# Low parts of the latent up-projection weights on VectorE, and every second head's diagonal blocks copied by ScalarE

## The chip, the cores and the metric

The kernel runs on one core of a Trainium2 chip. The metric is device time in microseconds (us); the time before is the median of three runs. Engines are called by their names or as the profile shortens them: TensorE (PE, and PEld for its weight loads), VectorE (DVE), ScalarE (ACT), GpSimd (POOL), SyncE (SP), which issues the loads.

## What is computed

Three transformer layers over 256 tokens of width 1024, in float32. Layer 1 mixes a gated linear recurrence, a gated linear attention and a block attention. Layers 2 and 3 (one function, called twice) each run three mixers side by side: a delta-rule recurrence (RWKV-7), a dilated local attention, and a latent attention (MLA). Every layer ends with an output projection and a gated FFN of width 2816. The lines that the change touches belong to these two parts of the reference:

```python
def step(state, inp):                      # delta rule, one token after another
    r_t, w_t, k_t, v_t, kk_t, b_t = inp
    sa = jnp.einsum('bhvk,bhk->bhv', state, kk_t)
    state = (state * w_t[:, :, None, :] - sa[..., None] * b_t[:, :, None, :]
             + v_t[..., None] * k_t[:, :, None, :])
    return state, jnp.einsum('bhvk,bhk->bhv', state, r_t)
...
q = (rms_norm_2(cq, q_norm_g) @ w_uq)      # latent attention: up-projections
kv = (rms_norm_2(ckv, kv_norm_g) @ w_ukv)
```

## The kernel before

**Weights.** Every large weight comes from memory as a float32 tile (`wraw`, three buffers, loads on SyncE's queue) and is split in two: ScalarE writes a rounded high part (`whi`, line 293), and the low part `wlo = wraw - whi` is made by VectorE (line 295) or, where the caller passes `G`, by GpSimd (line 297). Both parts have five buffers. A product is three matmuls: high by high, low by high, high by low. With 266 such splits the weights' path is a steady load of ScalarE and VectorE. GpSimd makes the low parts in `latent` and of the first three weights of each `out_proj`.

**The mixer of layers 2 and 3.** `layer2` writes the recurrence, the dilated and the latent attention as generators, and `lay` traces them in the order of the string `PLAN2`: `i` is the chain of the recurrence (`inverses`), `d` the dilated attention, `l` the latent attention, `c`, `v`, `o`, `u` the rest of the recurrence. The traced order gives each instruction its priority. A scheduler then gives each engine one fixed list of instructions; it takes the earliest in the traced order among those that it holds ready at that moment. Each engine works through its list strictly in order, and an instruction that waits holds up all behind it. PLAN2 begins `iciiiiiididlilli`: the setting up of the four weights of `latent` (in the first `l`) is traced after the block copies and before the first step of `solve`.

**The chain of the recurrence.** `inverses` scales keys and queries by decays: `kk` is multiplied by the learning rate (line 1248, VectorE, 128x512), `be` and `ka` follow (1249, 1256). `pairs` multiplies `be` with keys and queries on TensorE (line 1286), for two heads at a time and in two PSUM banks `r`; VectorE copies the masked result to `LN` (line 1291), after GpSimd has set it to zero (line 1290). Then the 32x32 blocks on the diagonal of each head's matrix are copied side by side into `Nd` (line 1264): four blocks for each of four heads, each copy 32 partitions x 64 elements, all by GpSimd. `solve` inverts the unit triangular matrices: line 1038 masks `Nd` into `Zd`, line 1039 transposes it to `Xd`, and then 32x32 products on TensorE (line 1035), ScalarE copies (1044) and masked VectorE copies (1048) double the inverted block size step by step.

**Beside it.** TensorE works in the same stretch on the dilated attention's projection (lines 472 to 475, the second half of the tokens) and then on the latent attention (lines 327 to 329). The high parts of three of the latent weights wait for buffers that the dilated projection still reads.

Of the kernel before, what the change touches and what calls it, by code (L numbers as in the profile page):

```python
# [13 lines left out]
AF = mybir.ActivationFunctionType  # L14
# [231 lines left out]
def tile_kernel(ctx: ExitStack, tc: tile.TileContext, a: dict, out: bass.AP, taps: dict = {}):  # L246
    nc = tc.nc
    V, A, G, PE = nc.vector, nc.scalar, nc.gpsimd, nc.tensor
# [9 lines left out]
    def bank(tag):  # L258
        return psum.tile([128, 512], F32, name="ps" + tag, tag="ps" + tag, bufs=BANKS[tag])
# [10 lines left out]
    def A1(name, shape, dt=F32):  # L270
        return T1(name, shape, dt, "a")
# [9 lines left out]
    def raw_weight(ap):  # L281
        raw = wpool.tile([128, ap.shape[1]], F32, name="wraw", tag="wraw", bufs=WB[0])
        nc.sync.dma_start(raw, ap)
        return raw

    def weight(ap, E=None):

        return split(raw_weight(ap), E)

    def split(raw, E=None):  # L290
        hi = wpool.tile([128, raw.shape[1]], F32R, name="whi", tag="whi", bufs=WB[1])
        lo = wpool.tile([128, raw.shape[1]], F32R, name="wlo", tag="wlo", bufs=WB[1])
        A.activation(hi, raw, AF.Copy)  # L293
        if E is None:
            V.tensor_sub(lo, raw, hi)  # L295
        else:
            E.tensor_tensor(lo, raw, hi, op=ALU.subtract)
        return hi, lo
# [26 lines left out]
    def mm3(o, xs, ws, start, stop):  # L325

        PE.matmul(o, xs[0], ws[0], start=start, stop=False)  # L327
        PE.matmul(o, xs[1], ws[0], start=False, stop=False)  # L328
        PE.matmul(o, xs[0], ws[1], start=False, stop=stop)  # L329
# [16 lines left out]
    def C(name):  # L346
        return found[name]
# [159 lines left out]
    def attention(score, bias, scale, v, h0, nh, dh, mixT, k0):  # L507


        n = 128 // dh  # L510

        def out_of(o, j):
            return o, j == 0, j == n - 1

        for i in range(0, nh, n):
            o = bank("o")[:, :256]
            for j in range(n):
                p = bank("s")
                score(h0 + i + j, p)
                softmax_head(p, bias(h0 + i + j), scale, v(h0 + i + j), *out_of(o, j))  # L520
                if j < n - 1:
                    yield
            m = [mx[:, k0 + i // n] for mx in mixT]
            A.activation(m[0], o, AF.Copy)
            V.tensor_sub(m[1], o, m[0])
            yield
# [170 lines left out]
    def halves(p):  # L697
        return p.rearrange("p (c t) -> p c t", c=2)

    def heads(ap, n):  # L700
        return ap.rearrange("p (h d) -> p h d", h=n)

    def hd(h, n=64):
        return slice(h * n, (h + 1) * n)
# [301 lines left out]
    def rotate(dst, src, nh, r, t, j0):  # L1006

        cb = rope["cos"][:, t, j0:j0 + r].unsqueeze(1).to_broadcast([128, nh, r])
        sb = rope["sin"][:, t, j0:j0 + r].unsqueeze(1).to_broadcast([128, nh, r])
        t1, t2 = src[:, :, :r], src[:, :, r:2 * r]  # L1010
        u = [heads(T0(f"ro{i}", [128, 128], 1)[:, :nh * r], nh) for i in range(4)]
        V.tensor_tensor(u[0], t1, cb, op=ALU.mult)
        V.tensor_tensor(u[1], t2, sb, op=ALU.mult)
        V.tensor_tensor(u[2], t1, sb, op=ALU.mult)
        V.tensor_tensor(u[3], t2, cb, op=ALU.mult)
        V.tensor_tensor(dst[:, :, :r], u[0], u[1], op=ALU.subtract)
        V.tensor_tensor(dst[:, :, r:2 * r], u[2], u[3], op=ALU.add)
# [135 lines left out]
    def recurrent(l, W, hT, mixT, last):  # L1153

        n = Names()
# [22 lines left out]
        def inverses():  # L1178
# [80 lines left out]
            for hp in range(2):  # L1259
                n.LN += pairs(n.be, hp, "LN", "r")  # L1260
                for h in (2 * hp, 2 * hp + 1):
                    for b in range(4):
                        bs = hd(b, 32)
                        G.tensor_copy(Nd[bs, :, h], n.LN[h][bs, :, 0, bs])
                yield
            Z = mix.tile([128, 8, 128], F32, name="Z", tag="Z", bufs=1)
            n.Z = Z.rearrange("p (c h) t -> p c h t", c=2)
# [14 lines left out]
        def pairs(src, hp, name, tag):  # L1282
            ps, ds = [bank(tag), bank(tag)], []
            for c in range(2):
                for j in range(2):
                    PE.matmul(ps[j][:, hd(c, 256)], src[hd(j), 2 * hp + c],
                              n.AR[hd(j), 2 * hp + c].rearrange("p a t -> p (a t)"), start=True, stop=True)
            for j in range(2):
                d = T2(name, [128, 2, 2, 128])
                G.memset(d, 0.0)  # L1290
                V.copy_predicated(d.rearrange("p b a t -> p b (a t)"), C("si").unsqueeze(1).to_broadcast([128, 2, 256]),
                                  halves(ps[j]))
                ds.append(d)
            return ds
# [70 lines left out]
        def outputs():  # L1365
# [59 lines left out]
            for t in range(2):  # L1425
                finish(t)
                yield

        return rest(), inverses(), values(), operands(), outputs()

    def dilated(l, W, hT, mixT, dv):
# [25 lines left out]
        yield from attention(score, lambda h: C("dil"), 0.125, lambda h: (dv[0][:, h], dv[1][:, h]), 0, 4, 64, mixT, 2)  # L1457

    def latent(l, mixT, cq, ckv, krT):
        wq = [[v.rearrange("p (k c) -> p k c", k=2) for v in weight(a[f"wuq_{l}"][:, s0:s0 + n], G)]  # L1460
              for s0, n in ((0, 1024), (1024, 512))]
        wk = [weight(a[f"wkv_{l}"][:, hd(i, 512)], G) for i in range(2)]
        room = [big.tile([128, 4, 512], F32, name=n, tag=n) for n in ("hTl", "hTh")]
        room = [v[:, i] for v in room for i in range(4)]
        take = lambda: halves(room.pop())
        qr = [take(), take()]
        for h in range(2):
            G.memset(qr[h][hd(1 - h)], 0.0)
        cv = []
        for t in range(2):  # L1470
            ts = hd(t, 128)
            p = bank("p")
            for k in range(2):
                mm3(p[:, :256], (cq[0][:, k, ts], cq[1][:, k, ts]), (wq[1][0][:, k], wq[1][1][:, k]), k == 0, k == 1)
            q = A1("qrt", [128, 256])
            rotate(heads(q, 4), heads(p[:, :256], 4), 4, 32, t, 8)
            pt = bank("t")
            for i in range(2):
                PE.transpose(pt[:, hd(i, 128)], q[:, hd(i, 128)], ident)
            for h in range(2):  # L1480
                V.tensor_copy(qr[h][hd(h), :, ts], heads(pt[hd(h), :256], 2))
            yield
            p = bank("p")
            mm3(p, (ckv[0][:, ts], ckv[1][:, ts]), wk[1], True, True)
            cv.append(room.pop())
            A.activation(cv[-1], p, AF.Copy)
            yield
        parts = []
        for h2 in range(2):
            p = bank("p")  # L1490
            for j in range(2):
                o, ws = p[:, hd(j, 256)], hd(2 * h2 + j, 128)
                for k in range(2):
                    wh, wl = wq[0][0][:, k, ws], wq[0][1][:, k, ws]
                    PE.matmul(o, wh, cq[0][:, k], start=(k == 0), stop=False)
                    PE.matmul(o, wh, cq[1][:, k], start=False, stop=False)
                    PE.matmul(o, wl, cq[0][:, k], start=False, stop=(k == 1))
            qn = take()
            V.tensor_copy(qn, halves(p))
            yield  # L1500
            p = bank("p")
            for j in range(2):
                o, ws = p[:, hd(j, 256)], hd(2 * h2 + j, 128)
                PE.matmul(o, wk[0][0][:, ws], ckv[0], start=True, stop=False)
                PE.matmul(o, wk[0][0][:, ws], ckv[1], start=False, stop=False)
                PE.matmul(o, wk[0][1][:, ws], ckv[0], start=False, stop=True)
            kn = take()
            A.activation(kn, halves(p), AF.Copy)

            parts.append((qn, kn))  # L1510
            yield
        for h2, (qn, kn) in enumerate(parts):

            def score(h, p):
                for q0, o, n in ((0, 0, 128), (128, 128, 256)):
                    PE.matmul(p[:, o:o + n], qn[:, h % 2, q0:q0 + 128], kn[:, h % 2, :n], start=True, stop=False)
                    PE.matmul(p[:, o:o + n], qr[h % 2][:, h2, q0:q0 + 128], krT[:, :n], start=False, stop=True)

            yield from attention(score, lambda h: C("causal"), 192.0 ** -0.5,
                      lambda h: (cv[0][:, hd(h, 128)], cv[1][:, hd(h, 128)]), 2 * h2, 2, 128, mixT, 4 + 2 * h2)  # L1520
# [59 lines left out]
```

## Time and profile before

| | |
|---|---|
| median of 3 runs | 1007.76 us (1007.62 to 1007.81) |
| profiled execution | 1007.09 us |
| its span, first to last instruction | 1004.9 us |
| busy: PE, DVE, ACT, POOL | 962.8, 655.0, 549.6, 88.5 us |
| granted TensorE clock, mean | 0.996 |

Busy times are sums over the span. The profile also has, for any stretch, the list of instructions of one engine in order of time with the idle time before each and what ended it, the busy time of all engines by stretch, and the chain of work that ended last, followed back from the end.

### The profile page before, as it was taken

What the parts mean: (1) busy time and instruction counts of PE and PEld (TensorE: products, weight loads), DVE (VectorE), ACT (ScalarE), POOL (GpSimd) and SP (SyncE); (2) the same over time, 40 slices, a digit from 0 to 9 for tenths busy, and PEclk for the clock granted to TensorE, in tenths of its full rate; (3) what the DMA queues carried; (4) which work ended last, traced back from release to release, by engine and by line L of the source; (5) the groups of instructions that cost most, each with busy time, mean ns of one, the idle gap of its engine ahead of it and who ended that gap; (6) DMA issues with size and microseconds to landing.
All of it is one profiled execution on the core that took longest, in us unless ns stands there. A gap on an engine that the chain in (4) does not pass through costs nothing.

```text
span 1004.9 us, 16830 instructions
## 1 busy us (share of the span) xinstructions
PE 962.8 (96%) x6551; PEld 817.7 (81%) x6551; DVE 655.0 (65%) x1212; ACT 549.6 (55%) x995; POOL 88.5 (9%) x125
## 2 busy tenths in 40 slices
PE   4998989999999998999999999999799999999997
PEld 3987878888887976888788888889688878888886
DVE  4777676666676687566666667666856576666663
ACT  5467565555565564455655555557255465555652
POOL 0003110000001122400000000010530000000000
PEclk9999999999999999999999999999999999999999
DMA  7863546666674623214565667635321246666751
GB/s 244 258 209 90 155 143 217 187 188 189 209 227 141 187 91 108 78 45 147 191 195 189 187 189 237 211 98 161 96 78 51 85 146 196 188 190 188 216 175 42
DMA packets 48635, 161.35 MB, mean 161 GB/s; under 512 B 5683, under 2 KB 9004, under 8 KB 48556
## 3 DMA queue, kind: packets, MB, share of 16 engines
q1 hardware_dynamic: 48556, 160.28, 51.7%
q8 instruction: 51, 0.84, 0.3%
q14 instruction: 28, 0.23, 0.1%
HBM read 159.20 MB, written 1.06 MB: 159 GB/s over the span
## 4 chain that ended last, share of the span: by engine, by line
PE 79%; DVE 10%; DMA 4%; ACT 3%; issue 2%; POOL 2%; SPq 0%; POOLq 0%; ACTq 0%; DVEq 0%
PE psp L462 9%; PE psr L462 9%; PE psp L463 5%; PE psr L463 5%; PE psp L449 3%; PE pss L328 3%; PE pss L329 3%; PE psp L450 3%; PE pss L327 3%; PE psp L451 3%; DMA wraw<-in_ffn_dram 3%; ACT whi L293 2%; PE psp L475 2%; PE psp L473 2%; PE pst L327 2%
## 5 line engine op out<-in xcount | busy, mean ns | idle before, releaser
L295 DVE TENSOR_TENSOR wlo<-wraw,whi 128x1024 fp32r<-128x1024 f32 (+2 forms) x249 | 301.6, 1214 | 171.4 <-ACT whi L293 168.3
L293 ACT ACTIVATE whi<-wraw 128x1024 fp32r<-128x1024 f32 (+3 forms) x266 | 275.7, 1039 | 231.7 <-PE psp L462 70.2
L462 PE MATMUL psp<-hTh,whi 128*128 128x512 f32 x228 | 82.9, 396 | 0.0
L462 PE MATMUL psr<-hTh,whi 128*128 128x512 f32 x228 | 82.6, 396 | 0.0
L462 PE MATMUL psp<-hTl,whi 128*128 128x512 f32 x228 | 82.5, 395 | 0.0
L462 PE MATMUL psr<-hTl,whi 128*128 128x512 f32 x228 | 82.5, 395 | 0.0
L463 PE MATMUL psp<-hTh,wlo 128*128 128x256 f32 x228 | 64.2, 282 | 0.0
L463 PE MATMUL psr<-hTh,wlo 128*128 128x256 f32 x228 | 64.0, 281 | 0.0
L463 PE MATMUL psp<-hTl,wlo 128*128 128x256 f32 x228 | 63.9, 280 | 0.0
L463 PE MATMUL psr<-hTl,wlo 128*128 128x256 f32 x228 | 63.8, 280 | 0.0
L631 ACT ACTIVATE sl<-cr 128x256 f32<-128x256 f32 x57 | 23.8, 417 | 57.6 <-DVE cr L629 57.5
L462 PEld LDWEIGHTS psr<-hTl,whi 128*128 128x128 f32 x228 | 42.8, 188 | 10.2
L462 PEld LDWEIGHTS psp<-hTl,whi 128*128 128x128 f32 x228 | 42.7, 187 | 10.1
L462 PEld LDWEIGHTS psr<-hTh,whi 128*128 128x128 f32 x228 | 42.8, 188 | 10.0
L462 PEld LDWEIGHTS psp<-hTh,whi 128*128 128x128 f32 x228 | 42.8, 188 | 9.8
L463 PEld LDWEIGHTS psp<-hTh,wlo 128*128 128x128 f32 x228 | 43.0, 189 | 3.1 <-DVE wlo L295 0.7
L629 DVE TENSOR_TENSOR cr<-psr,cr 128x256 f32<-128x256 f32 x57 | 24.1, 423 | 30.8 <-ACT cr L628 30.8
L463 PEld LDWEIGHTS psp<-hTl,wlo 128*128 128x128 f32 x228 | 43.0, 189 | 0.1
L463 PEld LDWEIGHTS psr<-hTl,wlo 128*128 128x128 f32 x228 | 43.1, 189 | 0.0
L463 PEld LDWEIGHTS psr<-hTh,wlo 128*128 128x128 f32 x228 | 43.1, 189 | 0.0
L449 PE MATMUL psp<-hTh,whi 128*128 128x256 f32 x144 | 42.0, 292 | 0.1
L450 PE MATMUL psp<-hTl,whi 128*128 128x256 f32 x144 | 41.6, 289 | 0.0
(673 smaller groups left out, 2395.6 us busy)
## 6 DMA issues: line engine op xcount, KB each, us to landing
wraw<-in_ffn_dram SPq DMA_DIRECT2D x198, 512.0 KB, 4.0
wraw<-in_win_dram SPq DMA_DIRECT2D x48, 512.0 KB, 4.1
wraw<-in_wout_dram SPq DMA_DIRECT2D x24, 512.0 KB, 3.6
gain<-in_prow_dram SPq DMA_DIRECT2D x9, 512.0 KB, 4.4
wraw<-in_win_dram SPq DMA_DIRECT2D x8, 480.0 KB, 4.3
wraw<-in_win_dram SPq DMA_DIRECT2D x4, 272.0 KB, 3.1
tb<-bdr SPq DMA_DIRECT2D x4, 256.0 KB, 3.8
wraw<-in_wuq_dram SPq DMA_DIRECT2D x2, 512.0 KB, 3.5
```

Source lines behind the costliest of these rows:

```text
L293: A.activation(hi, raw, AF.Copy)
L295: V.tensor_sub(lo, raw, hi)
L327: PE.matmul(o, xs[0], ws[0], start=start, stop=False)
L328: PE.matmul(o, xs[1], ws[0], start=False, stop=False)
L329: PE.matmul(o, xs[0], ws[1], start=False, stop=stop)
L449: PE.matmul(o, wh, hT[0][:, k, :], start=(k == 0), stop=False)
L450: PE.matmul(o, wh, hT[1][:, k, :], start=False, stop=False)
L451: PE.matmul(o, wl, hT[0][:, k, :], start=False, stop=(k == KC - 1))
L462: PE.matmul(o, wt[0][:, k], hT[2][k // 4][:, k % 4], start=(k == 0), stop=False)
L463: PE.matmul(o[:, S:], wt[1][:, k], hT[0][:, k, :], start=False, stop=(k == KC - 1))
L629: V.tensor_tensor(cr[:, i], p[:, :S], cr[:, i], op=ALU.add)
L631: n_.silu = A.activation(sl[:, 0], cr[:, 0], AF.Silu)
```

## The change

```diff
                 for h in (2 * hp, 2 * hp + 1):
                     for b in range(4):
                         bs = hd(b, 32)
-                        G.tensor_copy(Nd[bs, :, h], n.LN[h][bs, :, 0, bs])
+                        if h % 2:
+                            A.activation(Nd[bs, :, h], n.LN[h][bs, :, 0, bs], AF.Copy)
+                        else:
+                            G.tensor_copy(Nd[bs, :, h], n.LN[h][bs, :, 0, bs])
...
     def latent(l, mixT, cq, ckv, krT):
-        wq = [[v.rearrange("p (k c) -> p k c", k=2) for v in weight(a[f"wuq_{l}"][:, s0:s0 + n], G)]
+        wq = [[v.rearrange("p (k c) -> p k c", k=2) for v in weight(a[f"wuq_{l}"][:, s0:s0 + n])]
               for s0, n in ((0, 1024), (1024, 512))]
-        wk = [weight(a[f"wkv_{l}"][:, hd(i, 512)], G) for i in range(2)]
+        wk = [weight(a[f"wkv_{l}"][:, hd(i, 512)]) for i in range(2)]
```

In each of layers 2 and 3, four low parts (one of 128x1024, three of 128x512) are made on line 295 by VectorE instead of line 297 by GpSimd, and the eight block copies of heads 1 and 3 are ScalarE copies; those of heads 0 and 2 stay on GpSimd. The products, buffers and loads are the same.

## Rows read from the trace of the kernel before

**Rows 1.** The page: busy time, share of the span, instructions of each engine.
```profile
PE 962.8 (96%) x6551; PEld 817.7 (81%) x6551; DVE 655.0 (65%) x1212; ACT 549.6 (55%) x995; POOL 88.5 (9%) x125
```
**Rows 2.** Busy time by stretch, all engines; then granted clock, DMA share, GB/s.
```profile
364.00:372.00 8.00, 7.27 (x37) 5.56 (x35) 5.19 (x8) 4.73 (x10) 4.75 (x3) 1.00 0.12 34
372.00:382.00 10.00, 7.50 (x55) 5.41 (x59) 8.85 (x23) 1.15 (x2) 6.84 (x21) 1.00 0.11 27
...
470.00:660.00 190.00, 189.04 (x993) 159.89 (x992) 124.96 (x176) 106.81 (x175) 4.02 (x7) 1.00 0.62 193
...
700.00:720.00 20.00, 16.82 (x204) 12.54 (x202) 15.74 (x31) 6.27 (x13) 13.01 (x24) 1.00 0.14 36
```
**Rows 3.** TensorE in time order, 364 to 396: start, duration; idle before, releaser.
```profile
372.96 1.14 PE L1286 MATMUL psr<-AR,be 64*128 64x256 f32 x8 [1.51 <-DVE be L1249]
...
376.02 1.74 PE L1286 MATMUL psr<-AR,be 64*128 64x256 f32 x8 [0.56 <-DVE LN L1291]
...
381.84 0.74 PE L1035 MATMUL psr<-Xd,LN 32*32 32x32 f32 x64 [0.98 <-DVE Xd L1039]
...
387.79 0.32 PE L1035 MATMUL psr<-Xd,LN 32*32 32x32 f32 x13 [1.71 <-issue]
```
**Rows 4.** VectorE in time order, 369 to 385.
```profile
369.13 2.48 DVE L1248 SCALAR_TENSOR_TENSOR kk<-kk,av 128x512 f32<-128x512 f32 x1
...
375.25 1.32 DVE L1291 COPY_PREDICATED LN<-i,psr 128x512 f32<-128x512 int32 x2
...
377.25 1.35 DVE L1291 COPY_PREDICATED LN<-i,psr 128x512 f32<-128x512 int32 x2
378.50 0.83 DVE L1448 COPY dqT<-pst 64x256 f32<-64x256 f32 x2
380.44 0.45 DVE L1038 COPY_PREDICATED Zd<-i,Nd 128x256 f32<-128x256 int32 x1 [1.11 <-POOL Nd L1264]
...
381.26 0.43 DVE L1039 STREAM_TRANSPOSE Xd<-Zd 128x256 f32<-128x256 f32 x1
381.62 2.08 DVE L1320 SCALAR_TENSOR_TENSOR r__3702<-r__3702,pcol,k__3602 128x256 f32<-128x256 f32 x2
...
384.21 0.45 DVE L1048 COPY_PREDICATED Zd<-i,psr 128x256 f32<-128x256 int32 x1 [0.43 <-PE psr L1035]
```
**Rows 5.** GpSimd in time order, 368 to 387.
```profile
368.42 2.65 POOL L297 TENSOR_TENSOR wlo<-wraw,whi 128x1024 fp32r<-128x1024 f32 x1 [2.67 <-ACT whi L293]
...
376.03 4.38 POOL L1264 COPY Nd<-LN 32x64 f32<-32x64 f32 x16 [0.85 <-DVE LN L1291]
380.49 2.93 POOL L297 TENSOR_TENSOR wlo<-wraw,whi 128x512 fp32r<-128x512 f32 x2
```
**Rows 6.** ScalarE in time order, 367 to 401.
```profile
367.29 1.05 ACT L293 ACTIVATE whi<-wraw 128x1024 fp32r<-128x1024 f32 x1
...
379.30 1.15 ACT L293 ACTIVATE whi<-wraw 128x512 fp32r<-128x512 f32 x2 [7.44 <-PE psp L475]
...
398.51 1.69 ACT L1054 ACTIVATE Z<-Zd 32x256 f32<-32x256 f32 x4 [1.75 <-DVE Zd L1048]
```
**Rows 7.** VectorE groups, whole span: count, busy us, mean ns, idle before.
```profile
L295 DVE TENSOR_TENSOR wlo<-wraw,whi 128x1024 fp32r<-128x1024 f32 x237 | 289.5, 1224 | 163.4 <-ACT whi L293 160.3
...
L306 DVE TENSOR_TENSOR wv<-wraw,wv 128x512 fp32r<-128x512 f32 x8 | 5.5, 684 | 0.2 <-ACT wv L305 0.2
...
L1248 DVE SCALAR_TENSOR_TENSOR kk<-kk,av 128x512 f32<-128x512 f32 x2 | 5.0, 2476 | 0.0
...
L854 DVE SCALAR_TENSOR_TENSOR xc<-xp,pcol,xc 128x256 f32<-128x256 f32 x6 | 2.4, 467 | 0.0
...
L873 DVE SCALAR_TENSOR_TENSOR th<-rr,th 128x512 f32<-128x512 f32 x1 | 0.7, 683 | 0.0
```
**Rows 8.** ScalarE groups, whole span.
```profile
L1001 ACT ACTIVATE kq<-ang 128x80 f32<-128x80 f32 x1 | 0.3, 258 | 0.0
...
L1236 ACT ACTIVATE fs<-fs 128x2 f32<-128x2 f32 x2 | 0.4, 192 | 0.0
```

## The prediction

> **What bounds the kernel now.** I read the page's busy line first: TensorE is busy for 96% of the span, VectorE for 65%, ScalarE for 55%, GpSimd for 9% [rows 1]. GpSimd is nearly idle, so moving work off it pays only where it is waited for. The busy time by stretch says where that can be. In the FFN stretch, 470 to 660 us, TensorE has 189.04 busy of 190 us, and nothing is to be had. In 372 to 382 it has 7.50 of 10 [rows 2]. There VectorE is busy for 8.85 us and GpSimd for 6.84: the short stretch in which the recurrence prepares its matrix inverse. The same stretch of the next layer starts 336 us later (TensorE 16.82 of 20 us), and its rows repeat these within 0.1 us, so I work out one layer and double it.
>
> TensorE in order of time names the waits [rows 3]: 1.51 us for `be`, 0.56 us for the first copied `LN`, 0.98 us for `Xd`, 3.05 us in all. The 1.71 us that follow at 386.1 end in "issue", with no engine waited for. VectorE's list shows the chain behind the three waits [rows 4]: the product `kk` (line 1248) at 369.13 takes 2.48 us, then come `be`, the scalings, two masked copies at 375.25, two at 377.25, the mask of `Zd` at 380.44 after 1.11 us of waiting for GpSimd, and the transpose to `Xd` at 381.26.
>
> **Part 1: low parts off GpSimd.** GpSimd's low part of 128x1024 runs from 368.42 to 371.07 [rows 5], and `kk` on VectorE from 369.13 to 371.61 [rows 4]. A product of the same kind and size, both inputs also in SBUF, takes 683 ns elsewhere; both layers' `kk` average 2476 ns [rows 7]. `kk` ends 0.54 us after GpSimd does, so I read it as held up by GpSimd's instruction, and with that gone it should take 0.7 us. In the chain this is 2.48 - 0.7 = 1.75 us, of which I count 1.7. The floor is no gain, if `kk` is slow for a reason of its own; for the hold speaks that the two multiplications of line 1320 take 2.08 us for a pair [rows 4] beside GpSimd's next two low parts (380.49 to 383.41) [rows 5], where a 128x256 one costs 467 ns [rows 7].
>
> What `be` gains, TensorE gains up to its 1.51 us: it then meets no wait there, reaches the next pair of products at 375.46 - 1.51 = 373.95 and finds the first `LN` copied at 375.93 - 1.7 = 374.2. The shift of TensorE is 1.7 us from there on, and the masked copies at 377.25 come at 375.55.
>
> Added on VectorE per layer: one low part of 128x1024 at 1224 ns and three of 128x512 at 684 ns [rows 7], together 3.28 us. Against it stand 1.7 us at `kk` and 2.08 - 0.93 = 1.15 us at line 1320, so VectorE's sum grows by only 0.4 us; what matters is where the pieces stand in its list. The row that decides for me is line 1320. Its inputs come from the scalings ahead of the first masked copies, some 6 us before, and yet it stands behind the transpose at 381.26 [rows 4]: up to there the list held no opening for work traced later. The low parts are traced behind the masked copies and ahead of line 1320, so I expect them where line 1320 stands now, behind `Xd`. Ahead of it a 128x1024 part would cost the chain 1.22 us. Behind it, one that is under way when the next mask (line 1048, 384.21) is ready holds it up: between 0 and 1.22 us; I take 0.45 us, two thirds of the 684 ns of the commoner size. That wait TensorE would see at its third group of small products. The two 128x512 high parts start at 379.30 on ScalarE after 7.44 us of waiting for the dilated projection to release buffers [rows 6], so their low parts can't be ready before 379.9 now, or about 378.2 with TensorE 1.7 us earlier. TensorE's products with them come behind the dilated projection in its list, so they are in time.
>
> **Part 2: eight of sixteen block copies on ScalarE.** GpSimd copies without a break from 376.03 to 380.41, 0.27 us apart [rows 5], and the mask follows at once. The last `LN` (head 3) is ready at 377.25 + 1.35 = 378.60 [rows 4]. With the halves side by side, GpSimd does head 0 from 376.03 and head 2 from 377.93, done at 379.0; ScalarE does head 1 from 376.6, and head 3 from 378.62. Of ScalarE's price this trace has no row of 64 elements: between 192 ns (2 elements) and 258 ns (80) [rows 8], and four 32-partition copies of 256 elements in 1.69 us, 0.42 each, one behind the other [rows 6]. I take 0.26, the nearest in size, without overlap as in that row: head 3 is done at 379.66, against 380.41. The gain is 0.75 us; at 0.42 it is 0.1. ScalarE has nothing else to do from 372 until 379.30 [rows 6]. If the copies into one tile are ordered one after another across the two engines, each of head 3's still has its predecessor of head 2 done by 379.05, so that costs nothing. GpSimd's freed time is worth nothing beyond this.
>
> The ScalarE page of the Trainium skill ("ScalarE: Activation LUTs", What ACT_TABLE_LOAD costs) gives an activation with immediate operands 186 ns plus 0.833 ns per element, and says that neighbours overlap by some 93 ns; by estimate four copies would take 0.68 us instead of 1.04. The row of four copies in 1.69 us shows no such overlap for 32-partition pieces; by the page the sum would be 0.7 us better over both layers.
>
> **Sum.** The mask of `Zd` is due 1.7 + 0.75 = 2.45 us earlier, and so is `Xd`; TensorE, shifted by 1.7 us, arrives at 379.16 and waits until 379.39, so its first small products start 2.45 us earlier. Less the 0.45 us behind it: 2.0 us per layer, 4.0 in all. From there TensorE works through its list with few waits until the end, and what it gains it keeps [rows 2]. Against the profiled execution (1007.09 us: span 1004.9 and 2.2 around it) this gives 1003.1; the median of the runs lies 0.67 us above that execution, so I forecast 1003.8 us.
>
> **Rivals.**
> 1. *The low part of 128x1024 stands ahead of the mask.* `whi` is done at 368.34 [rows 6], before most of the chain; one opening in VectorE's list, between two dependent scalings, is enough. Then 2.45 - 1.22 = 1.23 us per layer remain: 1007.76 - 2.5 = 1005.3. Against it speaks line 1320's place.
> 2. *A low part blocks GpSimd's copies.* VectorE has now no large two-input SBUF instruction beside the `Nd` copies [rows 4, 5]; the change adds some. If one holds up head 2's copies as GpSimd held up `kk`, they come up to 1.22 us late, 0.6 of it hidden by ScalarE's later end: 1003.8 + 1.2 = 1005.0. The Trainium skill ("SBUF — State Buffer", Who interferes with whom) has it as a rule: a VectorE instruction with two SBUF inputs and a GpSimd one that reads SBUF exclude each other, and whichever starts second waits for the whole of the first. The 0.54 us between the ends of GpSimd's part and `kk` agree with it.
> 3. *The gain is given back.* TensorE waits 1.71 us with no engine named just behind [rows 3]; if its instructions arrive at a fixed pace, that wait takes what the others lose. The time stays within 1006 to 1008, say 1007.3. Against it: some 4 us of work lie between the last chain wait and that one.
> 4. *Slower: ScalarE's copies stand behind the two high parts.* Those wait for TensorE's buffers, until 379.30 - 1.7 = 377.6, and take 1.15 us [rows 6]. Eight copies from 378.75 end at 380.8 with 0.26 us each, at 382.1 with 0.42, which is 1.65 us later than now: 1007.76 + 3.3 = 1011.1. It decides from 0.21 us a copy against any gain, and from 0.33 against more than 0.2%. Against it: the high parts are traced later, and the first `LN` pair is ready 2.7 us before the buffers (376.57 against 379.30).
>
> **How the numbers follow.** Forecast 0.42, rival 1 0.21, rival 2 0.05, rival 3 0.20, rival 4 0.12. About 0.2%, 2.0 us, can be told from no change, so faster is below 1005.7: most of the forecast's 0.42 (0.41), seven tenths of rivals 1 and 2 (0.18), none of the others: 0.59. Slower is above 1009.8: rival 4 less its mild half, plus lists reordered elsewhere: 0.12. The rest, 0.29, is no change. The low end takes every engine wait of [rows 3] away, 3.05 us per layer: 1007.76 - 6.1 = 1001.7, and 0.2 us for the scatter of the runs: 1001.5. The high end takes in rival 3 and the mild half of rival 4: 1008.6.
>
> **What would show it.** `kk` at 0.7 us instead of 2.48; TensorE's 1.51 us for `be` gone; block copies on two engines, the mask of `Zd` some 0.75 us earlier behind the last `LN`; the four low parts behind the transpose to `Xd`; TensorE's first small products about 2.4 us earlier in each layer, with 0.2 us of waiting. I am wrong if `kk` stays slow, if a low part stands between `kk` and the mask (rival 1), if ScalarE's list has the high parts first (rival 4), or if the waits without an engine grow by what the others lose (rival 3).

## The result, and the profile after

The changed kernel takes 1014.78 us (median of 4 runs, 1013.24 to 1016.22), against 1007.69 us for the kernel before beside it (4 runs): a ratio of 1.0078, 95% interval 1.0057 to 1.0098. It is 0.8% slower. The forecast was 1003.8 us, with a range up to 1008.6: wrong, on the wrong side.

The profiled execution took 1016.22 us. Its engines are busy for almost what they were [rows 1], GpSimd for less and TensorE for 14 us more, with the same 6551 matmuls:

```profile
PE 976.7 (96%) x6551; PEld 830.7 (82%) x6551; DVE 655.4 (65%) x1220; ACT 553.8 (55%) x1011; POOL 71.7 (7%) x101
```

**Up to the first small products.** VectorE's list of the changed kernel in order of time answers to [rows 4] (from here on line numbers behind 1264 are 3 higher: 1291 is 1294):

```profile
369.83 0.68 DVE L1248 SCALAR_TENSOR_TENSOR kk<-kk,av 128x512 f32<-128x512 f32 x1
...
378.70 0.46 DVE L1038 COPY_PREDICATED Zd<-i,Nd 128x256 f32<-128x256 int32 x1
379.05 1.21 DVE L295 TENSOR_TENSOR wlo<-wraw,whi 128x1024 fp32r<-128x1024 f32 x1
380.18 0.44 DVE L1039 STREAM_TRANSPOSE Xd<-Zd 128x256 f32<-128x256 f32 x1
380.54 1.25 DVE L295 TENSOR_TENSOR wlo<-wraw,whi 128x512 fp32r<-128x512 f32 x2
381.71 0.87 DVE L1323 SCALAR_TENSOR_TENSOR r__3702<-r__3702,pcol,k__3602 128x256 f32<-128x256 f32 x2
```

`kk` takes 0.68 us and the pair of line 1323 takes 0.87, where they took 2.48 and 2.08. The mask no longer waits for GpSimd. But the wide low part stands between the mask and the transpose. GpSimd's and then ScalarE's copies, in order of time, answer to [rows 5, 6]:

```profile
374.93 1.09 POOL L1267 COPY Nd<-LN 32x64 f32<-32x64 f32 x4 [0.85 <-DVE LN L1294]
376.95 1.05 POOL L1267 COPY Nd<-LN 32x64 f32<-32x64 f32 x4 [0.93 <-DVE LN L1294]
```

```profile
375.51 1.05 ACT L1265 ACTIVATE Nd<-LN 32x64 f32<-32x64 f32 x4 [2.91 <-DVE LN L1294]
377.54 1.05 ACT L1265 ACTIVATE Nd<-LN 32x64 f32<-32x64 f32 x4 [0.99 <-DVE LN L1294]
378.62 1.15 ACT L293 ACTIVATE whi<-wraw 128x512 fp32r<-128x512 f32 x2
...
386.17 1.06 ACT L293 ACTIVATE whi<-wraw 128x1024 fp32r<-128x1024 f32 x1 [2.56 <-DMA wraw<-in_win_dram]
387.13 0.36 ACT L1044 ACTIVATE v<-psr 128x256 f32<-128x256 f32 x1
```

The copies are ahead of the high parts and cost 0.26 us each. The last two rows are new: the copy `v` of the inversion stands behind a split that waits 2.56 us for its load.

**From there on.** TensorE of the changed kernel in order of time, with the rows that answer to [rows 3]:

```profile
372.12 1.13 PE L1289 MATMUL psr<-AR,be 64*128 64x256 f32 x8
...
374.92 1.73 PE L1289 MATMUL psr<-AR,be 64*128 64x256 f32 x8 [0.31 <-DVE LN L1294]
...
380.83 0.75 PE L1035 MATMUL psr<-Xd,LN 32*32 32x32 f32 x64
...
387.55 0.75 PE L1035 MATMUL psr<-Zd,v 32*32 32x32 f32 x64 [1.28 <-ACT v L1044]
...
400.84 0.18 PE L1035 MATMUL psr<-Zd,v 32*32 32x32 f32 x1 [2.71 <-issue]
```

The wait of 1.51 us for `be` is gone, and so is the wait for `Xd`. Inside the groups of small products come a wait of 1.28 us for the `v` just seen and one of 2.71 that ends in "issue", where before had 1.71. And TensorE's clock falls. Busy time by stretch (the columns of [rows 2]: length, then PE, PEld, DVE, ACT, POOL; granted clock, DMA share, GB/s), first of the kernel before, then of the changed one:

```profile
382.00:396.00 14.00, 11.59 (x468) 9.33 (x462) 10.46 (x34) 5.03 (x11) 2.68 (x2) 1.00 0.50 153
396.00:470.00 74.00, 73.16 (x625) 61.91 (x616) 43.10 (x120) 37.52 (x85) 12.55 (x12) 1.00 0.29 85
```

```profile
382.00:396.00 14.00, 12.62 (x405) 10.28 (x405) 11.10 (x40) 4.51 (x10) 0.00 (x0) 0.88 0.51 166
396.00:470.00 74.00, 70.54 (x587) 59.86 (x574) 37.62 (x111) 34.58 (x80) 12.44 (x11) 0.88 0.20 64
401.00:419.00 18.00, 17.85 (x139) 15.39 (x139) 6.19 (x18) 8.75 (x18) 7.46 (x5) 0.53 0.18 60
743.00:757.00 14.00, 13.88 (x111) 11.80 (x110) 3.85 (x11) 5.12 (x10) 4.45 (x5) 0.51 0.21 67
```

A granted clock of 0.5 is the lower of the two levels, 1.2 GHz instead of 2.4. In 401 to 419 TensorE is "busy" for 17.85 of 18 us at about half of its speed: a full busy row does not say that an engine runs at speed. Summed over windows of 1 us (twice what each lacks to a clock of 1), in the three stretches of 100 us that hold the small products of the layers (from 60, 376 and 708 us), this execution ran 38 us at the lower level, the one before 3.4.

### The profile page after: what moved, and what is told of

It reads as the page before. It is cut to its first block, busy times and chain, and to the rows that moved or that the text cites. A ratio compares the mean times of both kernels' runs of the same rounds, so it can differ in the third digit from the quotient of the medians.

```text
span 1014.4 us, 16843 instructions
## 1 busy us (share of the span) xinstructions
PE 976.7 (96%) x6551; PEld 830.7 (82%) x6551; DVE 655.4 (65%) x1220; ACT 553.8 (55%) x1011; POOL 71.7 (7%) x101
## 4 chain that ended last, share of the span: by engine, by line
PE 77%; DVE 11%; ACT 4%; DMA 3%; issue 2%; POOL 2%; SPq 0%; POOLq 0%; ACTq 0%; DVEq 0%
PE psp L462 10%; PE psr L462 10%; PE psp L463 5%; PE psr L463 5%; PE pss L328 3%; PE pss L329 3%; PE pss L327 3%; PE psp L450 3%; PE psp L449 3%; PE psp L451 3%; DVE wlo L295 2%; ACT whi L293 2%; DMA wraw<-in_win_dram 2%; PE psp L475 2%; PE psp L472 2%
## 5 line engine op out<-in xcount | busy, mean ns | idle before, releaser
L295 DVE TENSOR_TENSOR wlo<-wraw,whi 128x1024 fp32r<-128x1024 f32 (+2 forms) x257 | 307.8, 1201 | 176.5 <-ACT whi L293 171.7
L463 PE MATMUL psp<-hTh,wlo 128*128 128x256 f32 x228 | 64.2, 281 | 0.0
L462 PEld LDWEIGHTS psr<-hTl,whi 128*128 128x128 f32 x228 | 42.7, 187 | 10.2
L462 PEld LDWEIGHTS psp<-hTl,whi 128*128 128x128 f32 x228 | 42.7, 187 | 10.1
L451 PE MATMUL psp<-hTh,wlo 128*128 128x256 f32 x144 | 42.2, 293 | 1.4 <-issue 1.4
```

The source lines that it names most:

```text
L451: PE.matmul(o, wl, hT[0][:, k, :], start=False, stop=(k == KC - 1))
L462: PE.matmul(o, wt[0][:, k], hT[2][k // 4][:, k % 4], start=(k == 0), stop=False)
L463: PE.matmul(o[:, S:], wt[1][:, k], hT[0][:, k, :], start=False, stop=(k == KC - 1))
```

## The experiments

The ideas at the start: the two parts together shift the lists and with them TensorE's waits and clock; or the low parts on VectorE cost by holding the raw buffers longer; or the earlier small products by themselves bring the clock down, whatever made them earlier.

**Each part alone.** `low_only` makes only the low parts on VectorE, `copy_only` only splits the copies, and `first_low_copy` splits the copies and moves the 128x1024 low part alone:

```diff
# low_only: the changed kernel, with
+                        G.tensor_copy(Nd[bs, :, h], n.LN[h][bs, :, 0, bs])
# copy_only: the kernel before, with
+                        if h % 2:
+                            A.activation(Nd[bs, :, h], n.LN[h][bs, :, 0, bs], AF.Copy)
# first_low_copy: the changed kernel, with
+ weight(a[f"wuq_{l}"][:, s0:s0 + n], None if s0 == 0 else G)
+ weight(a[f"wkv_{l}"][:, hd(i, 512)], G)
```

Expected of `low_only`: 

> The change's first part alone: the four low parts of the latent weights per layer on VectorE, all sixteen block copies left on GpSimd. Theory 1 (the clock: the changed kernel brings the products of the block inverse closer together, waits at other places, and TensorE's clock falls to 1.2 GHz behind them; the copies on ScalarE are what reorders the lists): the lists of this kernel are nearly those of before, the multiplication of line 1248 takes 0.7 us instead of 2.48, the clock stays where it was (mean 0.99 or more), and the time is 2 to 4 us below before. Theory 2 (the low parts: they stand late in VectorE's list and hold the load buffers some 9 us longer, so that loads and ScalarE's splits come late and hold up the chain): slower than before by 3 us or more, with the loss between 380 and 435 us.

Expected of `copy_only`: 

> The change's second part alone: eight of sixteen block copies per layer on ScalarE, the low parts left on GpSimd. Theory 1: the lists change much as in the changed kernel, the chain to the first small products is 0.7 us shorter, and behind it the clock falls and the time is 3 to 7 us above before. Theory 2: no low part moves, the load buffers are released as before, so 1 to 2 us faster than before, with the clock at 0.99 or more.

Expected of `first_low_copy`: 

> The changed kernel with only the first low part (128x1024) of the four on VectorE, the three of 128x512 back on GpSimd; the copies are split between GpSimd and ScalarE. Its lists are close to those of the changed kernel. Theory 1: slow like the changed kernel, 1012 to 1016 us, with two stretches at half the clock behind 385 and 735 us. Theory 2, the buffers held by the wide low part: slow as well; if it is the three narrow ones: near before.

| kernel | median us (runs) | ratio to before, 95% interval |
|---|---|---|
| low_only | 1000.92 (4) | 0.9945, 0.9927 to 0.9962 |
| copy_only | 1003.43 (10) | 0.9972, 0.9951 to 0.9994 |
| first_low_copy | 1014.33 (4) | 1.0071, 1.0044 to 1.0098 |

Each part alone makes the kernel faster, by 6.2 and 3.7 us against the 1007.16 of before on that chip; together they make it 7 slower. Both lie outside every range that I had written down for them: `low_only` gained more than 2 to 4 us, and `copy_only` neither lost 3 to 7 nor gained 1 to 2. The low parts are no cost by themselves, so the second idea falls as it stands. `kk` confirms its reading: in the groups of VectorE by line it is, in `low_only` and then in `copy_only`,

```profile
L1248 DVE SCALAR_TENSOR_TENSOR kk<-kk,av 128x512 f32<-128x512 f32 x2 | 1.4, 682 | 0.0
```

```profile
L1248 DVE SCALAR_TENSOR_TENSOR kk<-kk,av 128x512 f32<-128x512 f32 x2 | 4.9, 2470 | 0.0
```

682 ns without GpSimd's low part beside it and 2470 with it, on the same inputs. In `first_low_copy` TensorE runs at a clock of 0.76 in 382 to 396.

**Keeping TensorE at work.** `after_warm` puts a product that nobody reads at the head of each group of small products, `after_warm2` also at the five later groups of a layer:

```diff
         def diagonal(lhs, rhs, p):
+            PE.matmul(p[:, 256:], ident, C("dil"), start=True, stop=True)
```

Expected of `after_warm`: 

> The changed kernel with one extra 128x256 product ahead of each of the sixteen groups of small products (eight per layer) in the block inverse, into columns of the same bank that nobody reads; some 0.3 us of TensorE each, 2.4 us per layer. Theory 1: TensorE stays busy with large products, the clock stays at 0.99 or more, and in spite of the extra work it is faster than the changed kernel by 3 us or more. Theory 2: the clock is not the cause, so it is slower than the changed kernel by up to 5 us.

Expected of `after_warm2`: 

> The changed kernel with an extra 128x256 product not only ahead of the sixteen groups of 32x32 products per two layers, as in the run with eight per layer, but also ahead of the five later groups of the block inverse in each layer; none of their results is read. Theory 1: with the eight the clock held until 400 us and fell behind it, where the later groups run; with these it holds there too (0.99 or more in the mean), and the time is below 1008 us in spite of some 3.5 us of extra work per layer. If the clock's falls have nothing to do with what TensorE executes there: as with eight, 1009 to 1013 us, with 15 us or more at the lower clock.

`after_warm` took 1010.71 us (10 runs; 1.0038, 1.0022 to 1.0054), `after_warm2` 1012.28 (10 runs; 1.0048, 1.0024 to 1.0072). Busy time by stretch of `after_warm`:

```profile
382.00:396.00 14.00, 14.00 (x495) 11.13 (x495) 9.86 (x32) 4.57 (x8) 0.00 (x0) 1.00 0.49 153
...
388.00:392.00 4.00, 4.00 (x142) 3.06 (x140) 3.94 (x12) 0.39 (x1) 0.00 (x0) 1.00 0.45 145
...
404.00:408.00 4.00, 4.00 (x21) 4.00 (x20) 0.44 (x2) 1.06 (x1) 0.00 (x0) 0.52 0.02 4
```

The clock held where it had fallen in the changed kernel (0.57 in 388 to 392), and fell later all the same. In `after_warm2` it held until 419, and the mean over the span of the profiled execution was 0.997; but the added products cost time themselves (32 of their 52 instructions are 9.9 us of TensorE's busy time), and the time stayed above the 1008 us that I had expected if the clock held. Neither run is the changed kernel with its waits filled: the edit gave new lists here too. In the order of TensorE's weight loads, as the traces have it, 264 of the changed kernel's 6551 stand elsewhere in `after_warm`, and ScalarE's second `v` stands ahead of the split that it stood behind:

```profile
384.85 0.38 ACT L1045 ACTIVATE v<-psr 128x256 f32<-128x256 f32 x1 [3.64 <-PE psr L1036]
...
386.29 1.05 ACT L293 ACTIVATE whi<-wraw 128x1024 fp32r<-128x1024 f32 x1
```

So these two runs don't show what the added products do to the clock, and neither says how much of the loss is clock and how much is waits.

**The same work with other heads on ScalarE.** Both parts stay; what changes is the condition:

```diff
-                        if h % 2:
+                        if h % 2 == 0:      # both_even: heads 0, 2
+                        if h >= 2:          # both_hp1: heads 2, 3
+                        if h == 3:          # both_h3
+                        if h < 3:           # both_h012
+                        if h in (1, 2):     # both_h12
```

Expected of `both_even`: 

> Both parts of the change, but ScalarE copies the blocks of heads 0 and 2 and GpSimd those of 1 and 3: the same instructions of the same sizes on each engine as in the changed kernel, in other lists (TensorE's list is close to that of the copies-alone kernel, 246 lines of difference, and far from the changed kernel's, 602). Theory 1, now: each part gains, and what the changed kernel loses comes from the one list of TensorE that their sum happens to give, with waits after which the clock falls for some 38 us in all. Then this kernel takes 998 to 1003 us, with less than 15 us at the lower clock. Theory 3: the two parts together shorten the chain so much that TensorE meets its small products close together whatever the list, and the clock falls: 1011 to 1016 us.

Expected of `both_hp1`: 

> Both parts, but ScalarE copies the blocks of heads 2 and 3 and GpSimd those of 0 and 1. TensorE's and ScalarE's lists are those of the changed kernel to the line; only the masks' wait for the copies moves: head 2 and 3 on one engine end about 1 us later than with a copy each. Theory 1: the list decides, so slow, 1011 to 1016 us, with the same stretches of the lower clock. Theory 3: the small products start about 1 us later, so the loss is partly undone, 1007 to 1012 us.

| kernel | median us (runs) | ratio to before, 95% interval |
|---|---|---|
| both_even | 999.43 (10) | 0.9924, 0.9900 to 0.9947 |
| both_hp1 | 1017.19 (10) | 1.0082, 1.0056 to 1.0109 |

The third idea falls too: `both_even` starts its small products 10.2 us behind the start of `kk`, earlier than the changed kernel's 11.0, and is the fastest so far. The lists without their times gave the next question. With both parts, every choice of heads that was run leads to one of two TensorE lists: call it list A if head 3 is copied by ScalarE (as in the changed kernel), list B if not (as in `both_even`, and in `low_only`, which copies no head there). In a line-by-line comparison of TensorE's 6551 weight loads in the order of the traces, 248 stand elsewhere in A than in B. List B is nearly that of before (30 stand elsewhere), and so is that of `copy_only` (16); `first_low_copy` has list A but for 30. The last four kernels test whether the list decides, with the changed kernel repeated beside the others as `after_again`.

Expected of `after_again`: 

> The changed kernel once more (heads 1 and 3 copied by ScalarE), as the yardstick beside the three others. Both theories: 1013 to 1016 us.

Expected of `both_h3`: 

> Both parts, with head 3 alone copied by ScalarE. Compared as lists of instructions, every kernel with both parts has one of two TensorE lists: one if head 3 is copied by ScalarE (the changed kernel, heads 2 and 3), the other if it is not (heads 0 and 2, or all copies on GpSimd). Theory A, the list decides: 1011 to 1017 us, with TensorE below full clock for some 25 us or more in all behind 386 us and 737 us, although only four copies a layer are moved. Theory B, the number of copies on ScalarE or the engines' work decides: between low parts alone (1000.9) and heads 0 and 2 (999.4), so 999 to 1002.

Expected of `both_h012`: 

> Both parts, heads 0, 1 and 2 copied by ScalarE, head 3 by GpSimd: twelve copies on ScalarE, the other of the two TensorE lists. Theory A, the list decides: 998 to 1002 us, with at most 10 us below full clock. Theory B, ScalarE's copies are what costs: more than the changed kernel's 1014.8.

Expected of `both_h12`: 

> Both parts, heads 1 and 2 copied by ScalarE: eight copies as in the changed kernel, one head of each pair as there, and the TensorE list of heads 0 and 2. Theory A, the list decides: 998 to 1001 us. Theory B, which engine ends last on a pair or the work on the engines decides: 1012 to 1016, since the engines' work is that of the changed kernel.

| kernel | list | copies on ScalarE per layer | median us (runs) | ratio to before, 95% interval |
|---|---|---|---|---|
| after_again | A | 8 | 1014.33 (6) | 1.0075, 1.0047 to 1.0103 |
| both_h3 | A | 4 | 1017.28 (5) | 1.0086, 1.0045 to 1.0127 |
| both_h012 | B | 12 | 998.89 (10) | 0.9927, 0.9905 to 0.9950 |
| both_h12 | B | 8 | 999.89 (4) | 0.9934, 0.9908 to 0.9960 |

The list decides: the medians fall on the side that it forecast, though `both_hp1` and `both_h3` lie 1.2 and 0.3 us above their ranges. Four copies on ScalarE with list A cost 0.9%; twelve with list B gain 0.7%. `both_h12` does on each engine what the changed kernel does, and is 14.4 us faster on the same chip. `both_h012` and `both_even` beat both given kernels. Head 3 on ScalarE is no cost by itself, since `copy_only` has it there too and gains. "The list" means the lists of all engines: VectorE's and ScalarE's change along with TensorE's, and no run changes one of them alone.

**What differs in list A.** VectorE of `both_even` in order of time has the low parts where the prediction put them, behind the transpose:

```profile
375.83 0.46 DVE L1038 COPY_PREDICATED Zd<-i,Nd 128x256 f32<-128x256 int32 x1 [0.41 <-POOL Nd L1267]
...
376.66 0.43 DVE L1039 STREAM_TRANSPOSE Xd<-Zd 128x256 f32<-128x256 f32 x1
377.02 2.39 DVE L295 TENSOR_TENSOR wlo<-wraw,whi 128x1024 fp32r<-128x1024 f32 x3
```

In list A the wide low part comes between the two, `Xd` is due 1.2 us later, and TensorE's list has five more large products (lines 472, 473 and 475) ahead of the first small ones. ScalarE's `v` stands ahead of the split that waits for its load in list B, not behind it. The load itself is no later in list A: the split starts 16.3 us behind the start of `kk` in the changed kernel and 16.4 in `both_even`, so it is the order that holds `v` up. Again `both_even`:

```profile
382.61 0.38 ACT L1044 ACTIVATE v<-psr 128x256 f32<-128x256 f32 x1
383.45 1.06 ACT L293 ACTIVATE whi<-wraw 128x1024 fp32r<-128x1024 f32 x1 [0.47 <-DMA wraw<-in_win_dram]
```

TensorE of `both_h12` (list B), then of `after_again` (list A), whose clock was 1.00 in the whole stretch:

```profile
378.17 0.74 PE L1035 MATMUL psr<-Xd,LN 32*32 32x32 f32 x64 [0.29 <-DVE Xd L1039]
...
382.12 0.74 PE L1035 MATMUL psr<-Xd,LN 32*32 32x32 f32 x64 [0.27 <-DVE Xd L1049]
...
387.30 0.44 PE L1035 MATMUL psr<-Xd,LN 32*32 32x32 f32 x28 [0.62 <-issue]
...
394.41 0.74 PE L1060 MATMUL psr<-Xd,LN 32*32 32x32 f32 x16
```

```profile
378.99 0.75 PE L1035 MATMUL psr<-Xd,LN 32*32 32x32 f32 x64
...
385.23 0.75 PE L1035 MATMUL psr<-Zd,v 32*32 32x32 f32 x64 [1.09 <-ACT v L1044]
...
396.36 0.18 PE L1035 MATMUL psr<-Zd,v 32*32 32x32 f32 x1 [2.07 <-issue]
...
397.74 0.69 PE L1060 MATMUL psr<-Xd,LN 32*32 32x32 f32 x16
```

From the first product of line 1035 to the first of line 1060, its eight groups take 16.2 us in list B and 18.8 in list A, at the same clock. The stretches of both, `both_h12` first:

```profile
382.00:396.00 14.00, 13.08 (x450) 11.26 (x451) 11.79 (x43) 7.47 (x17) 0.00 (x0) 1.00 0.54 187
396.00:470.00 74.00, 73.09 (x511) 61.26 (x510) 43.81 (x113) 38.99 (x85) 12.84 (x12) 1.00 0.28 85
```

```profile
382.00:396.00 14.00, 11.20 (x428) 9.36 (x428) 11.27 (x40) 4.90 (x13) 0.00 (x0) 1.00 0.51 166
...
396.00:470.00 74.00, 72.33 (x511) 60.93 (x511) 42.80 (x109) 37.51 (x81) 13.01 (x12) 0.98 0.23 78
```

**Waits and clock apart.** I take the time from the first product with `be` to the first of line 1083 (the last group of the inversion) in each profiled execution, and the time at 1.2 GHz within it:

| kernel, list | layer 2: us, of it at 1.2 GHz | layer 3: us, of it at 1.2 GHz |
|---|---|---|
| before | 52.92, 0 | 54.10, 3.4 |
| both_h12, B | 50.77, 0 | 52.27, 3.4 |
| both_even, B | 52.35, 3.4 | 52.55, 3.4 |
| both_h012, B | 54.75, 6.8 | 51.48, 0 |
| after_again, A | 53.51, 3.4 | 59.40, 17.1 |
| after, A | 61.33, 20.5 | 57.03, 13.7 |
| both_hp1, A | 57.77, 10.2 | 61.35, 20.5 |
| both_h3, A | 61.91, 20.5 | 61.73, 23.9 |

A straight line through the eight values of list A gives 52.4 us at full clock (standard error 0.8) and 0.42 us more for each microsecond at the lower level (largest miss 1.2 us); through the six of list B, 50.9 us (0.3) and 0.50 (largest miss 0.5). By this, list A costs about 1.5 us a layer by its waits, and the rest by the clock: for the changed kernel (20.5 + 13.7) x 0.42 = 14.4 us, where before lost 3.4 x 0.42 = 1.4. The page "TensorE: Matmul & The Clock Gate" of the Trainium skill (Terms) puts the penalty of a clock at half rate at half of the time spent there; the two slopes lie near that.

Each run also has its span and its mean granted clock, so the same can be done with all of them: 60 runs of before, 25 of the four kernels with list A, 28 of the four with list B. The mean clock was 0.985 to 0.999 in those of before, 0.988 to 0.999 with list B, and 0.977 to 0.988 with list A; as time at 1.2 GHz over the whole span, 9.5, 7.7 and 36.3 us on average. So the loss of clock belongs to list A and not to the one execution that was profiled. One slope for all three, with a level for each, gives 0.35 us per microsecond (95% interval 0.30 to 0.40). At equal clock list B is then 6.6 us faster than before (6.0 to 7.2) and list A 1.2 (-0.2 to 2.6). List A loses 15.5 us on list B: 5.4 by its waits, 2.7 a layer, and 10.1 by the clock. The two workings differ on the waits and agree that the larger part of the loss is clock.

## Why the prediction was wrong

**Right.** `kk` at 0.7 us (0.68), the wait for `be` gone, line 1323's pair at 0.87. The kernel now reaches the first product with `be` 1.54 us earlier, counted from `kk` (372.12 - 369.83 = 2.29, before 372.96 - 369.13 = 3.83); I had 1.51 to 1.7 (2.48 - 0.7 is 1.78, not the 1.75 that I wrote; the sum counts 1.7 and doesn't change). Also counted from `kk`, the mask of `Zd` comes 2.44 us earlier (378.70 - 369.83 = 8.87, before 380.44 - 369.13 = 11.31), where I had 2.45. The rule of "SBUF — State Buffer" of the Trainium skill (Who interferes with whom) fits: VectorE's product with two SBUF inputs is held as long as GpSimd's runs, and no longer when that is gone.

**Right.** ScalarE's copies at 0.26 us, ahead of the high parts, so rival 4 did not come. The overlap that "ScalarE: Activation LUTs" of the Trainium skill (What ACT_TABLE_LOAD costs) gives, 0.68 us for four by estimate, is not seen: 1.05 us for four, as the row of four copies [rows 6] had it. GpSimd's copies were not held up (1.09 and 1.05 us for four), so rival 2 did not come either.

**Half right.** The low parts stand behind `Xd` in list B, as forecast, and the wide one ahead of it in list A: rival 1. I priced that at 1.22 us a layer on VectorE's chain. TensorE met no wait for `Xd`, because its list had put more large products ahead of the small ones: these start 1.71 us earlier than before, counted from `kk` (380.83 - 369.83 = 11.00, before 381.84 - 369.13 = 12.71), where I had 2.45. In `both_even` they start 2.5 us earlier. Rival 3's wait without an engine grew to 2.71 us in list A, but shrank to 0.62 in list B, so it is no fixed pace that takes back what the others lose.

**The step that failed** is the sentence "From there TensorE works through its list with few waits until the end, and what it gains it keeps". It held two things fixed that the change moves: which list TensorE has, and its clock, which has no term in the sum at all. I reckoned the path of before with some durations taken out, where the scheduler wrote a new list for every engine; of TensorE's weight loads 252 stand elsewhere than before. That list has its waits in the small products, 1.28 us for `v` and 2.71 for "issue"; and in the profiled execution 34 us of the two inversions ran at 1.2 GHz. My 0.12 for slower held "lists reordered elsewhere" as a remainder without a price.

The sum by these terms, for the profiled executions: -1.5 us per layer at `kk`, 52.4 - 52.9 = -0.5 from there at full clock, so -4.0 in all; then 14.4 - 1.4 = +13.0 by the clock: +9.0, measured 1016.22 - 1007.09 = +9.1. This closes better than it should: the line was fitted to these executions too, and the two timed stretches grew by 11.3 us, not 12.0, while 1.2 us of the difference lie outside them. That -4.0 is also the sum I had forecast is chance: it hangs on the 52.4, and all runs together give -1.2 at equal clock. With list B it is -1.5 and 50.9 - 52.9 = -2.0 per layer, -7.0 in all, and the four kernels that have it gained 6.2 to 7.8. So the forecast was short there: both parts gained 6.4 to 7.8 where I had 4.0, and the first part alone 6.2 where 1.7 - 0.45 per layer make 2.5. The wait without an engine, which I had left at 1.71 us, is part of that. In list B the change is 0.7% faster.

**What stays open.** Why the clock falls where it does. The changed kernel fell at 388 in one execution (clock 0.57 in 388 to 392) and held 1.00 there until 416 in another, with the same list and nearly the same waits (1.28 and 1.09 us for `v`). The falls come inside or behind the groups of small products. In `after_warm` TensorE was busy for 14.00 of 14 us in 382 to 396, and the clock fell behind 400 all the same, but its list is another. That the waits start the falls is a guess that the runs neither show nor exclude. Whether the held `v` or the five large products weigh more in list A wasn't tried apart, nor what made the scheduler choose list A.

## What to carry to other kernels

Where a scheduler writes the lists, a small edit is two changes: the one that the diff shows, and a new list. Compare the lists of before and after before trusting a sum made on the old path, and try a neutral variant (here: which heads go to ScalarE) to separate the two; it was worth 14 us, about twice what the edit itself gained. Read the granted clock beside every busy share, since an engine at half its clock shows as fully busy.

## What the runs showed of the hardware

At the lower clock a 128x256 product of line 449 has a duration of 0.41 us instead of 0.28 in the changed kernel's trace. The changed kernel had 38 us at 1.2 GHz in one profile and 20.5 in another, summed over the three stretches of small products (1016.22 and 1009.62 us). At 0.42 us per microsecond the 17.1 us between them make 7.2 us; the times differ by 6.6. List B's profiled executions had 3 to 10 us of it.
